# Gate and up products of a feed-forward block by Strassen's seven block products, in two groups of tokens

## The chip, the cores and the metric

The kernel runs on one core of a Trainium2 chip. The metric is the device time of one execution in microseconds (us). The core's engines are TensorE (PE, matrix products; PEld is its weight load), VectorE (DVE), ScalarE (ACT), GpSimd (POOL) and SyncE (SP, which here only issues DMA transfers). Each engine works its own instructions in order; semaphores tie the engines together. Matrix products accumulate in PSUM, all other tiles lie in SBUF.

## What is computed

One step of a streaming encoder layer for 1072 tokens (16 + 1024 + 32) of width 1024: two kinds of attention, an output projection, and a SwiGLU feed-forward part of hidden width 2816. Only the end of it is touched by the change:

```
def finish_layer(x, mixed, w_out, norm_ffn, w_gate, w_up, w_down):
    x = x + mixed @ w_out                     # second half of it in the stage looked at here
    h = rms_norm(x, norm_ffn)
    return x + (jax.nn.silu(h @ w_gate) * (h @ w_up)) @ w_down
y = rms_norm(finish_layer(...), final_norm)
```

Everything is in float32. A float32 factor is split into a high part and a low part of a shorter format (`split`, L65 to L67: ScalarE writes hi by a copy, VectorE writes lo as source minus hi), and one product is three matmuls: hi·hi, hi·lo, lo·hi (`mm3`, L117 to L121).

## The kernel before

Tokens lie along the columns. After attention, the stage `C` (from L770) holds the residual stream as `x2` and does, in this order: the second half of the output projection (L804 to L823, `psG<-A_hi,woh`), the operands of the feed-forward part (h without its per-token factor, as hi and lo in the four big tiles `A_hi`, `A_lo`, `B_hi`, `B_lo`, L829 and L830), the feed-forward part, and the last norm with the output.

The feed-forward part walks over 22 blocks f of 128 hidden units. Tokens stand in three chunks of 408, 408 and 256. For a block and a chunk `gate_up` issues 24 matmuls for the gate and 24 for the up product (eight slices of the 1024-wide contraction, three matmuls each), multiplies both by the token's norm factor `rb` (L849, L854), applies silu on ScalarE, multiplies (L855) and splits the result into `ah` and `al`. Then `down` works on the block before it: for each of eight output slices three matmuls into a PSUM tile `psD` (L861 to L863) and one VectorE addition of it to `x2` (L870). Gate, up and down share a ring of six PSUM tiles (`psG`, 2 KB per partition each). The weights of a block come by three transfers of 512 KB from SyncE's queue (L57), and are split in pieces of 1024 columns, one block ahead. GpSimd has no part in this until the last block, where it adds squares (L801) and scales outputs (L894).

What sets the order: engines run in program order, and a scheduler, which places the instructions of the loops above on each engine, has fixed it before the run. Tiles are taken from rings (`bufs`); an instruction that writes a tile waits for the last reader of the tile that stood there before.

## Time and profile before

| | |
|---|---|
| time, median of 3 runs | 1568.96 us (1565.36 to 1571.4) |
| the profiled execution | 1569.29 us |
| its span, first to last instruction | 1567.5 us |
| TensorE busy | 1494.9 us, 95% |
| VectorE busy | 978.5 us, 62% |
| ScalarE, GpSimd busy | 594.6 us, 215.8 us |
| TensorE's granted clock over the span | 0.99 of full speed |

The time of a run is 1.8 us longer than the span. Busy shares are averages over the attention part (up to about 716 us) and the stage `C` behind it; what holds in a stage is read from windows of that stage. A matmul's duration in the profile is longer than the distance to the next one, since matmuls overlap; the rate of TensorE is read from the distance between starts.

### The profile page before, as it was taken

What the parts mean: (1) busy time and instruction counts of PE and PEld (TensorE: products, weight loads), DVE (VectorE), ACT (ScalarE), POOL (GpSimd) and SP (SyncE); (2) the same over time, 40 slices, a digit from 0 to 9 for tenths busy, and PEclk for the clock granted to TensorE, in tenths of its full rate; (3) what the DMA queues carried; (4) which work ended last, traced back from release to release, by engine and by line L of the source; (5) the groups of instructions that cost most, each with busy time, mean ns of one, the idle gap of its engine ahead of it and who ended that gap; (6) DMA issues with size and microseconds to landing.
All of it is one profiled execution on the core that took longest, in us unless ns stands there. A gap on an engine that the chain in (4) does not pass through costs nothing.

```text
span 1567.5 us, 24204 instructions
## 1 busy us (share of the span) xinstructions
PE 1494.9 (95%) x9273; PEld 1432.9 (91%) x9273; DVE 978.5 (62%) x1843; ACT 594.6 (38%) x1204; POOL 215.8 (14%) x343
## 2 busy tenths in 40 slices
PE   7999998988898999998999999999999999999995
PEld 6999997777786988888999999999999999999995
DVE  8965535667767776775945556555655655655647
ACT  7444336666755665664612111111111111111124
POOL 1244141423232122110000000000000000000014
PEclk9999999999999999999999999999999999999998
DMA  6588666766867667625201111111111121111003
GB/s 192 172 279 277 198 205 203 249 200 176 237 205 205 176 162 189 165 84 187 62 28 41 46 63 55 41 41 41 41 41 41 41 64 54 45 41 41 27 1 113
DMA packets 88467, 185.27 MB, mean 118 GB/s; under 512 B 9818, under 2 KB 53786, under 8 KB 88260
## 3 DMA queue, kind: packets, MB, share of 16 engines
q1 hardware_dynamic: 71424, 129.44, 28.9%
q0 software_dynamic: 16928, 54.29, 9.9%
q8 instruction: 73, 1.20, 0.3%
q14 instruction: 42, 0.34, 0.1%
HBM read 125.02 MB, written 58.67 MB: 117 GB/s over the span
## 4 chain that ended last, share of the span: by engine, by line
PE 80%; DVE 6%; DMA 5%; ACT 4%; issue 3%; POOL 1%; DVEq 0%; SPq 0%; ACTq 0%; POOLq 0%
PE psG L120 11%; PE psG L119 11%; PE psG L121 11%; PE psD L862 5%; PE psD L863 5%; PE psD L861 5%; PE psS L568 4%; PE psT L630 3%; PE psA L121 3%; PE psA L119 3%; PE psA L120 3%; PE po L646 2%; PE po L647 1%; DMA sK<-es 1%; PE psG L816 1%
## 5 line engine op out<-in xcount | busy, mean ns | idle before, releaser
L870 DVE TENSOR_TENSOR x<-psD,x 128x408 f32<-128x408 f32 (+1 forms) x496 | 236.7, 524 | 5.7 <-PE psD L863 5.7
L119 PE MATMUL psG<-B_hi,gh 128*128 128x408 f32 (+1 forms) x528 | 172.8, 327 | 0.0
L119 PE MATMUL psG<-A_hi,gh 128*128 128x408 f32 (+1 forms) x528 | 172.6, 327 | 0.0
L120 PE MATMUL psG<-A_lo,gh 128*128 128x408 f32 (+1 forms) x528 | 172.6, 327 | 0.0
L120 PE MATMUL psG<-B_lo,gh 128*128 128x408 f32 (+1 forms) x528 | 172.5, 327 | 0.0
L863 PE MATMUL psD<-ah,dl 128*128 128x408 f32 (+1 forms) x528 | 172.1, 326 | 0.0
L121 PE MATMUL psG<-B_hi,gl 128*128 128x408 f32 (+1 forms) x528 | 171.8, 325 | 0.0
L121 PE MATMUL psG<-A_hi,gl 128*128 128x408 f32 (+1 forms) x528 | 171.8, 325 | 0.0
L862 PE MATMUL psD<-al,dh 128*128 128x408 f32 (+1 forms) x528 | 171.7, 325 | 0.0
L861 PE MATMUL psD<-ah,dh 128*128 128x408 f32 (+1 forms) x528 | 170.9, 325 | 0.1
L850 ACT ACTIVATE sl<-sl 128x408 f32<-128x408 f32 (+1 forms) x66 | 33.1, 503 | 354.6 <-DVE sl L849 354.6
L854 DVE TENSOR_TENSOR sq<-psG,rb 128x408 f32<-128x408 f32 (+1 forms) x66 | 35.0, 530 | 152.2 <-PE psG L121 152.1
L801 POOL TENSOR_TENSOR acc<-acc,sq 128x408 f32<-128x408 f32 x14 | 15.0, 1070 | 810.5 <-ACT sq L800 809.9
L571 DVE TENSOR_REDUCE nm<-psS 128x1 f32<-128x656 f32 (+2 forms) x144 | 104.2, 725 | 31.0 <-PE psS L568 29.8
L67 DVE TENSOR_TENSOR ptl<-psT,pth 128x512 fp32r<-128x512 f32 x192 | 104.2, 553 | 30.1 <-ACT pth L66 27.8
L66 ACT ACTIVATE pth<-psT 128x512 fp32r<-128x512 f32 (+4 forms) x208 | 98.5, 480 | 56.5 <-PE psT L630 49.4
L568 PE MATMUL psS<-b,a 128*128 128x328 f32 (+4 forms) x360 | 103.4, 338 | 9.1 <-ACT pb L576 5.5
L849 DVE TENSOR_TENSOR sl<-psG,rb 128x408 f32<-128x408 f32 (+1 forms) x66 | 35.0, 530 | 123.2 <-PE psG L121 123.2
L66 ACT ACTIVATE ah<-sl 128x408 fp32r<-128x408 f32 (+1 forms) x66 | 33.2, 503 | 188.5 <-DVE sl L855 121.4
L120 PEld LDWEIGHTS psG<-A_lo,gh 128*128 128x128 f32 x528 | 99.3, 188 | 0.5 <-issue 0.3
L861 PEld LDWEIGHTS psD<-ah,dh 128*128 128x128 f32 x528 | 99.2, 188 | 0.5 <-ACT ah L66 0.3
L119 PEld LDWEIGHTS psG<-A_hi,gh 128*128 128x128 f32 x528 | 99.2, 188 | 0.5 <-issue 0.2
(272 smaller groups left out, 3825.5 us busy)
## 6 DMA issues: line engine op xcount, KB each, us to landing
sg<-w_gu SPq DMA_DIRECT2D x44, 512.0 KB
a<-sQ SPq DMA_DIRECT2D x56, 268.0 KB
b<-sK SPq DMA_DIRECT2D x32, 396.0 KB
sg<-w_down SPq DMA_DIRECT2D x22, 512.0 KB
v<-sV SPq DMA_DIRECT2D x16, 512.0 KB
wst<-w_in SPq DMA_DIRECT2D x13, 512.0 KB
sV<-vt POOLq DMA_DIRECT2D x24, 256.0 KB, 3.9
sV<-A_hi POOLq DMA_DIRECT2D x24, 256.0 KB, 2.9
```

Of the source, the lines that this page charges most:

```text
L66: act.activation(hi, src, AF.Copy)
L67: eng.tensor_tensor(out=lo, in0=src, in1=f32(hi), op=ALU.subtract)
L119: pe.matmul(ps, whi(k), rhi(k), start=(k == 0), stop=False)
L120: pe.matmul(ps, whi(k), rlo(k), start=False, stop=False)
L121: pe.matmul(ps, wlo(k), rhi(k), start=False, stop=(k == K - 1))
L568: pe.matmul(out, qa[:K, t0:t0 + nq], kb[:K, k0 + c:k0 + c + w], start=(j == 0), stop=last)
L571: dve.tensor_reduce(out=nm[:nq, j:j + 1], in_=src, axis=AX.XY if len(src.shape) == 3 else AX.X, op=ALU.max, negate=True)
L630: pe.transpose(out=pt[:, 128 * g:128 * g + 128], in_=tiles[g][1][:, c:c + 128], identity=ident)
L861: pe.matmul(ps, dh[:, m], ah[:, cs], start=first and j == 0, stop=False)
L862: pe.matmul(ps, dh[:, m], al[:, cs], start=False, stop=False)
L863: pe.matmul(ps, dl[:, m], ah[:, cs], start=False, stop=last and j == len(parts) - 1)
L870: dve.tensor_tensor(out=x2[:, m, cs], in0=ps[:, :n], in1=x2[:, m, cs], op=ALU.add)
```

## The change

The matrix pair (gate, up) of a block is taken as a two-by-two block matrix: the contraction is halved (512 and 512), the outputs are gate and up, and the tokens are halved. Strassen's scheme (in Winograd's form) gives the four blocks of the result by seven block products in place of eight, with sums of blocks before and behind.

- Tokens are worked in two groups g of G = 536, each of two quarters of N = 268; a unit is a pair (g, f), so there are 44 units, and each block's weights are loaded twice.
- `w_sum` builds five of the seven weight operands of a unit by a GpSimd addition of two SBUF tiles (128x512, L811); two operands are the raw weights. `w_split` splits all seven, 512 columns each (hi in `gh` or `woh`, lo in `gl` or `wol`). The sums stand in the ring `wst` of two tiles. Both run about one unit ahead of the products (`ahead`).
- `h_make` writes the normalised h to SBUF and to DRAM; `h_first` and `h_last` build the seven token operands from it, the latter after the tiles `A_hi`, `A_lo` have been read for the last time as inputs of the output projection. For the second group this is done again at the end of the first one (`h_again`).
- `gate_up` issues seven products of 12 matmuls of 268 columns, in four PSUM tiles, and combines them (L981 to L1008); `ag` is the unit's result, and its split makes `ah` and `al`.
- `down` works on pairs of blocks, accumulated in PSUM: 48 matmuls, eight evictions (L1027) in a step, one step after each unit from f = 2 on. Its PSUM tiles `psD` are a ring of two of their own.
- The output projection goes by groups too; its eight weight tiles are loaded and split a second time. The end norms each quarter by itself (`final`).

```diff
@@ -508,9 +508,9 @@
     w_ring, w_next = [], [0]
 
     def out_weights(upto):
-        while w_next[0] < min(upto, 16):
+        while w_next[0] < min(upto, 24):
             stg, hi, lo = (wp.tile([128, 512], t, tag=g, name=g) for t, g in ((F32, "wst"), (FR, "woh"), (FR, "wol")))
-            load(stg.rearrange("p (k n) -> p k n", k=4), a["w_out"][w_next[0]])
+            load(stg.rearrange("p (k n) -> p k n", k=4), a["w_out"][w_next[0] if w_next[0] < 16 else w_next[0] - 8])
...
-        psN = C.enter_context(tc.tile_pool(name="psNF", bufs=2, space=PSUM))
+        psD = C.enter_context(tc.tile_pool(name="psD", bufs=2, space=PSUM))
+        N = T // 4
+        G = 2 * N
...
+        def w_sum(n):
+            if n >= 7 * len(units):
+                return
+            f, q = units[n // 7][1], n % 7
+            if q == 0:
+                up, gate = (wf.tile([128, 8, 128], F32, tag="sg", name="sg", bufs=3) for _ in range(2))
+                load(up, a["w_gu"][f, :, 1])
+                load(gate, a["w_gu"][f, :, 0])
+                raw[0] = (gate[:, 0:4], gate[:, 4:8], up[:, 0:4], up[:, 4:8])
+            a11, a12, a21, a22 = raw[0]
+            if q in (1, 2):
+                sums[n] = a11 if q == 1 else a22
+                return
+            x, y, op = {0: (a21, a22, ALU.add), 3: (a11, a12, ALU.add), 4: (a11, a22, ALU.add),
+                        5: (a21, a11, ALU.subtract), 6: (a12, a22, ALU.subtract)}[q]
+            s = wp.tile([128, 512], F32, tag="wst", name="wst").rearrange("p (k n) -> p k n", k=4)
+            pool.tensor_tensor(out=s, in0=x, in1=y, op=op)
+            sums[n] = s
+        def w_split(n):
+            if n >= 7 * len(units):
+                return
+            if n % 4 == 3:
+                hi, lo = (wp.tile([128, 512], FR, tag=t, name=t) for t in ("woh", "wol"))
+            else:
+                hi, lo = (wf.tile([128, 512], FR, tag=t, name=t, bufs=6) for t in ("gh", "gl"))
+            hi, lo = (t.rearrange("p (k n) -> p k n", k=4) for t in (hi, lo))
+            split(hi, lo, sums.pop(n))
+            quads[n] = (hi, lo)
...
+        def d_split(k):
+            if k >= len(steps):
+                return
+            _, p, h = steps[k]
+            sg = wf.tile([128, 2, 4, 128], F32, tag="dsg", name="dsg", bufs=1)
+            hi, lo = (wf.tile([128, 2, 4, 128], FR, tag=t, name=t) for t in ("dh", "dl"))
+            for j in range(2):
+                load(sg[:, j], a["w_down"][2 * p + j, :, 4 * h:4 * h + 4])
+            for j in range(2):
+                split(hi[:, j], lo[:, j], sg[:, j])
+            dws[k] = (hi, lo)
...
-                    for k in range(8):
-                        hi, lo = (t[:, k % 4, cs] for t in big[k // 4])
-                        act.activation(hi, x2[:, k, cs], AF.Copy, scale=g_ffn[:, k:k + 1])
-                        dve.scalar_tensor_tensor(lo, x2[:, k, cs], g_ffn[:, k:k + 1], f32(hi), ALU.mult, ALU.subtract)
-                    ps = psN.tile([128, 512], F32, tag="psn", name="psn")
-                    pe.matmul(ps[:, :n], ones, acc[:, cs], start=True, stop=True)
-                    rsqrt(rb[:, cs], ps, n, D, sqp)
...
+        def h_make(g, k):
+            h = ap_.tile([128, 2, G], F32, tag="hn", name="hn", bufs=2)
+            for j in range(2):
+                kk = k + 4 * j
+                dve.scalar_tensor_tensor(h[:, j], x2[g][:, kk], g_ffn[:, kk:kk + 1], accs[g], ALU.mult, ALU.mult)
+            put(sH[k, :, :, G * g:G * g + G], h)
+            return h
...
+        def h_first(h, k):
+            ct = ap_.tile([128, 3, N], F32, tag="ct", name="ct", bufs=1)
+            b = h.rearrange("p j (c n) -> p (j c) n", c=2)
+            dve.tensor_tensor(out=ct[:, 0], in0=b[:, 1], in1=b[:, 3], op=ALU.subtract)
+            dve.tensor_tensor(out=ct[:, 1], in0=b[:, 2], in1=b[:, 0], op=ALU.subtract)
+            yield
+            split(hB[0][:, 0:4:3, k], hB[1][:, 0:4:3, k], b[:, 0:4:3])
+            yield
+            split(hB[0][:, 1:3, k], hB[1][:, 1:3, k], ct[:, 0:2])
+            yield
+        def h_last(h, k):
+            ct = ap_.tile([128, 3, N], F32, tag="ct", name="ct", bufs=1)
+            b = h.rearrange("p j (c n) -> p (j c) n", c=2)
+            dve.tensor_tensor(out=ct[:, 0], in0=b[:, 0], in1=b[:, 3], op=ALU.add)
+            pool.tensor_tensor(out=ct[:, 1:3], in0=h[:, :, 0:N], in1=h[:, :, N:G], op=ALU.add)
+            yield
+            split(hA[0][:, 0:2, k], hA[1][:, 0:2, k], ct[:, 0:2])
+            yield
+            split(hA[0][:, 2, k], hA[1][:, 2, k], ct[:, 2])
+            yield
+        def h_again():
+            h = [h_load(1, 0)]
+            for k in range(4):
+                if k < 3:
+                    h.append(h_load(1, k + 1))
+                yield from h_first(h[k], k)
+                yield from h_last(h[k], k)
...
-            t1 = ap_.tile([128, 408], F32, tag="sl", name="sl")
-            t2 = sqp.tile([128, 408], F32, tag="sq", name="sq", bufs=2)
-            ps = product(0)
-            dve.tensor_tensor(out=t1[:, :n], in0=ps[:, :n], in1=rb[:, cs], op=ALU.mult)
-            silu[0] = act.activation(t1[:, :n], t1[:, :n], AF.Silu).ins
-            if between is not None:
-                between()
-            ps = product(1)
-            dve.tensor_tensor(out=t2[:, :n], in0=ps[:, :n], in1=rb[:, cs], op=ALU.mult)
-            dve.tensor_tensor(out=t1[:, :n], in0=t1[:, :n], in1=t2[:, :n], op=ALU.mult)
-            split(ah[:, cs], al[:, cs], t1[:, :n])
...
+        def gate_up(u):
+            g, f = units[u]
+            n0 = 7 * u
+            def product(ps, q, first):
+                hi, lo = quads.pop(n0 + q)
+                bh, bl = (t[:, q] for t in hB) if q < 4 else (t[:, q - 4] for t in hA)
+                for k in range(4):
+                    pe.matmul(ps[:, :N], hi[:, k], bh[:, k], start=first and k == 0, stop=False, skip_group_check=True)
+                    pe.matmul(ps[:, :N], hi[:, k], bl[:, k], start=False, stop=False, skip_group_check=True)
+                    pe.matmul(ps[:, :N], lo[:, k], bh[:, k], start=False, stop=(k == 3), skip_group_check=True)
+            def bank():
+                return psG.tile([128, 512], F32, tag="psG", name="psG")
+            def tmp(name):
+                return sqp.tile([128, N], F32, tag=name, name=name)
+            def ahead(q):
+                w_split(n0 + 7 + q)
+                w_sum(n0 + 8 + q)
+            pa, pb = bank(), bank()
+            product(pa, 0, True)
+            p0 = tmp("p0")
+            act.activation(p0, pa[:, :N], AF.Copy)
+            ahead(0)
+            product(pb, 1, True)
+            d = tmp("d")
+            dve.tensor_tensor(out=d, in0=pb[:, :N], in1=p0, op=ALU.subtract)
+            ahead(1)
+            product(pa, 2, False)
+            ahead(2)
+            product(pb, 3, False)
+            pc = bank()
+            product(pc, 4, True)
+            p4 = tmp("p4")
+            act.activation(p4, pc[:, :N], AF.Copy)
+            w = tmp("w")
+            dve.tensor_tensor(out=w, in0=pa[:, :N], in1=d, op=ALU.add)
+            dve.tensor_tensor(out=w, in0=w, in1=pb[:, :N], op=ALU.subtract)
+            g1 = tmp("g1")
+            silu[0] = act.activation(g1, pb[:, :N], AF.Silu).ins
+            ahead(3)
+            pd = bank()
+            product(pd, 5, True)
+            pool.tensor_tensor(out=d, in0=d, in1=p4, op=ALU.add)
+            ahead(4)
+            product(pc, 6, False)
+            ahead(5)
+            t = tmp("t")
+            dve.tensor_tensor(out=t, in0=pd[:, :N], in1=d, op=ALU.add)
+            dve.tensor_tensor(out=w, in0=pc[:, :N], in1=w, op=ALU.add)
+            act.activation(w, w, AF.Silu)
+            ag = sqp.tile([128, G], F32, tag="ag", name="ag")
+            dve.tensor_tensor(out=ag[:, N:G], in0=g1, in1=t, op=ALU.mult)
+            dve.tensor_tensor(out=ag[:, 0:N], in0=pa[:, :N], in1=w, op=ALU.mult)
+            ah, al = (t[:, f % 2] for t in (odd if f // 2 % 2 else spare))
+            split(ah, al, ag)
+            ahead(6)
+        def down(k, cs=(0, 1), norm=False, beside=iter(())):
+            g, p, h = steps[k]
+            dh, dl = dws[k]
+            ah, al = odd if p % 2 else spare
+            for c in cs:
+                for i in range(4):
+                    m = 4 * h + i
+                    ps = psD.tile([128, 512], F32, tag="psD", name="psD")
+                    for j in range(2):
+                        bh, bl = (t[:, j, N * c:N * c + N] for t in (ah, al))
+                        pe.matmul(ps[:, :N], dh[:, j, i], bh, start=(j == 0), stop=False)
+                        pe.matmul(ps[:, :N], dh[:, j, i], bl, start=False, stop=False)
+                        pe.matmul(ps[:, :N], dl[:, j, i], bh, start=False, stop=(j == 1))
+                    xs2 = x2[g][:, m, N * c:N * c + N]
+                    dve.tensor_tensor(out=xs2, in0=ps[:, :N], in1=xs2, op=ALU.add)
+                    if norm:
+                        square(g, m, c, pool if g == 0 else dve)
+                    next(beside, None)
...
+        for u, (g, f) in enumerate(units):
+            gate_up(u)
+            if g == 0 and f < 4:
+                h_make(1, f)
+            if f < 2 or f == 20:
+                continue
+            beside = iter(())
+            if f == 21 and g == 0:
+                beside = h_again()
+            for _ in range(1 if f < 20 else 2 if g == 1 else 4):
+                d_split(k + 1)
+                down(k, norm=f == 21 and steps[k][1] == NFF // 2 - 1, beside=beside)
+                k += 1
+            for _ in beside:
+                pass
+            if g == 1 and f in (2, 3):
+                final(0, f - 2)
+        d_split(k + 1)
+        for c in range(2):
+            down(k, (c,), norm=True)
+            down(k + 1, (c,), norm=True)
+            final(1, c)
```

TensorE around the seam between the products and the down step of a steady unit. Before, the down product of a chunk follows the last matmul of the up product; `DVE_49` and `Activation_49` are the semaphores of VectorE and ScalarE:

```order
L121 MATMUL psG<-B_hi,gl 128x408
L119 MATMUL psG<-B_hi,gh 128x408
L120 MATMUL psG<-B_lo,gh 128x408
L121 MATMUL psG<-B_hi,gl 128x408
L861 MATMUL psD<-ah,dh 128x408 [waits DVE_49,Activation_49]
L862 MATMUL psD<-al,dh 128x408
L863 MATMUL psD<-ah,dl 128x408
L861 MATMUL psD<-ah,dh 128x408 [waits DVE_49]
L862 MATMUL psD<-al,dh 128x408
```

Now, the piece from the end of the second `psD` tile of a step on, in the same view:

```order
L1025 MATMUL psD<-A_hi,dl 128x268
L960 MATMUL psG<-B_hi,woh 128x268
L961 MATMUL psG<-B_lo,woh 128x268
L962 MATMUL psG<-B_hi,wol 128x268
L960 MATMUL psG<-B_hi,woh 128x268
L961 MATMUL psG<-B_lo,woh 128x268
L1023 MATMUL psD<-A_hi,dh 128x268 [waits DVE_49]
L1024 MATMUL psD<-A_lo,dh 128x268
L1025 MATMUL psD<-A_hi,dl 128x268
L1023 MATMUL psD<-A_hi,dh 128x268
```

Two `psD` tiles are filled, five matmuls of the next unit's first product are drawn ahead, and the third `psD` tile waits for VectorE, which must have evicted the first.

VectorE in a stretch of the feed-forward part before, across the seam between two blocks (`x_8587` is the residual stream, `sg` a block's weights):

```order
L67 TENSOR_TENSOR dl<-sg,dh 128x1024
L870 TENSOR_TENSOR x_8587<-psD,x_8587 128x256
L67 TENSOR_TENSOR gl<-sg,gh 128x1024
L849 TENSOR_TENSOR sl<-psG,rb 128x408
L67 TENSOR_TENSOR gl<-sg,gh 128x1024
L854 TENSOR_TENSOR sq<-psG,rb 128x408
L870 TENSOR_TENSOR x_8587<-psD,x_8587 128x408
L855 TENSOR_TENSOR sl<-sl,sq 128x408
L870 TENSOR_TENSOR x_8587<-psD,x_8587 128x408 x2
L67 TENSOR_TENSOR al<-sl,ah 128x408
```

VectorE now, in one steady unit from the first combination behind product 2 on to the eviction of the first `psD` tile (`wst` are sums of weights from GpSimd, `psG` the products, `d` the tile to which GpSimd adds product 4):

```order
L991 TENSOR_TENSOR w_10937<-psG_10854,d_10886 128x268
L67 TENSOR_TENSOR wol_10943<-wst_10908,woh_10942 128x512
L992 TENSOR_TENSOR w_10937<-w_10937,psG_10855 128x268
L67 TENSOR_TENSOR gl_10963<-wst_10946,gh_10962 128x512
L67 TENSOR_TENSOR gl_10981<-wst_10966,gh_10980 128x512
L1003 TENSOR_TENSOR t_10986<-psG_10948,d_10886 128x268
L67 TENSOR_TENSOR gl_10996<-wst_10984,gh_10995 128x512
L1007 TENSOR_TENSOR ag_10990<-g1_10940,t_10986 128x268
L1004 TENSOR_TENSOR w_10937<-psG_10922,w_10937 128x268
L67 TENSOR_TENSOR wol_11095<-wst_11003,woh_11094 128x512
L1008 TENSOR_TENSOR ag_10990<-psG_10854,w_10937 128x268
L1027 TENSOR_TENSOR x20_8587<-psD_11014,x20_8587 128x268
```

Five low splits of weight sums stand between the combinations: four of the next unit, and one of the unit after it (`wol_11095`) just ahead of the last combination. The eviction of `psD` comes behind all of them.

GpSimd, which had nothing to do in the blocks before the last one, now works this sequence in the same unit, the last two rows being for the unit after the next:

```order
L811 TENSOR_TENSOR wst_10779<-sg_10775 128x512
L811 TENSOR_TENSOR wst_10908<-sg_10776 128x512
L811 TENSOR_TENSOR wst_10946<-sg_10776,sg_10775 128x512
L811 TENSOR_TENSOR wst_10966<-sg_10775,sg_10776 128x512
L811 TENSOR_TENSOR wst_10984<-sg_10776,sg_10775 128x512
L998 TENSOR_TENSOR d_10886<-d_10886,p4_10935 128x268
L811 TENSOR_TENSOR wst_11003<-sg_10999 128x512
L811 TENSOR_TENSOR wst_11132<-sg_11000 128x512
```

The unit's addition into `d` (L998) stands behind all five of a unit's weight sums, and the next sums follow it at once.

## Rows read from the trace of the kernel before

**Rows 1.** The page, part 1: busy time, share of the span and instructions of each engine

```profile
PE 1494.9 (95%) x9273; PEld 1432.9 (91%) x9273; DVE 978.5 (62%) x1843; ACT 594.6 (38%) x1204; POOL 215.8 (14%) x343
```

**Rows 2.** One stretch of the FFN by windows: busy us, instructions, clock, DMA share, GB/s

```profile
900.00:1000.00 100.00, 100.00 (x607) 99.81 (x606) 54.97 (x105) 16.05 (x24) 0.00 (x0) 1.00 0.15 48
```

**Rows 3.** SyncE's queue by time, 1005 to 1045 us: start us, us, engine, transfer

```profile
1007.10 0.33 SPq L57 DMA_DIRECT2D sg<-w_down  x1
1012.16 29.15 SPq L57 DMA_DIRECT2D sg<-w_gu  x2
1042.45 0.33 SPq L57 DMA_DIRECT2D sg<-w_down  x1
```

**Rows 4.** TensorE by time: the first matmul of the stage

```profile
716.73 0.42 PE L816 MATMUL psG<-A_hi,woh 128*128 128x408 f32 x1 [1.36 <-DVE raw L691]
```

**Rows 5.** TensorE by time: the last matmul of the last down product

```profile
1548.17 0.28 PE L863 MATMUL psD<-ah,dl 128*128 128x256 f32 x1
```

**Rows 6.** TensorE by time, matmuls of 256 and of 408 columns: start us, us, name

```profile
1000.38 0.28 PE L861 MATMUL psD<-ah,dh 128*128 128x256 f32 x1
...
1003.09 0.28 PE L863 MATMUL psD<-ah,dl 128*128 128x256 f32 x1
1003.21 0.35 PE L119 MATMUL psG<-A_hi,gh 128*128 128x408 f32 x1
...
1012.15 0.35 PE L861 MATMUL psD<-ah,dh 128*128 128x408 f32 x1
```

**Rows 7.** A window of 1 us behind the load issued at 1012.16 (columns as in rows 2)

```profile
1015.00:1016.00 1.00, 1.00 (x7) 1.00 (x6) 1.00 (x3) 0.00 (x0) 0.00 (x0) 1.00 0.11 45
```

**Rows 8.** All engines by time, 468.4 to 471 us: GpSimd and VectorE side by side

```profile
468.86 1.27 POOL L67 TENSOR_TENSOR wol<-wst,woh 128x512 fp32r<-128x512 f32 x1 [2.48 <-ACT woh L66]
469.14 1.38 DVE L504 TENSOR_TENSOR et<-et,et 128x358 f32<-128x358 f32 x1
```

**Rows 9.** VectorE groups by shape, 690 to 1568 us: count, busy us, mean ns, idle before

```profile
L870 DVE TENSOR_TENSOR x<-psD,x 128x408 f32<-128x408 f32 x336 | 176.6, 575 | 5.7 <-PE psD L863 5.7
L870 DVE TENSOR_TENSOR x<-psD,x 128x256 f32<-128x256 f32 x160 | 60.1, 418 | 0.0
L67 DVE TENSOR_TENSOR wol<-wst,woh 128x512 fp32r<-128x512 f32 x6 | 4.1, 686 | 0.1
```

**Rows 10.** VectorE and GpSimd by time, 1549 to 1554.5 us

```profile
1549.78 0.98 DVE L914 TENSOR_TENSOR acc<-acc,sq 128x512 f32<-128x512 f32 x1
1552.03 1.53 DVE L914 TENSOR_TENSOR acc<-acc,sq 128x512 f32<-128x512 f32 x1
...
1548.14 7.66 POOL L894 TENSOR_TENSOR x<-x,acc 128x408 f32<-128x408 f32 x6 [9.56 <-DVE acc L115]
```

**Rows 11.** GpSimd groups by shape, the whole span

```profile
L801 POOL TENSOR_TENSOR acc<-acc,sq 128x408 f32<-128x408 f32 x14 | 15.0, 1070 | 810.5 <-ACT sq L800 809.9
L67 POOL TENSOR_TENSOR wol<-wst,woh 128x512 fp32r<-128x512 f32 x10 | 13.0, 1302 | 28.0 <-ACT woh L66 27.9
```

**Rows 12.** VectorE and GpSimd by time, 1523 to 1526 us

```profile
1523.21 0.58 DVE L870 TENSOR_TENSOR x<-psD,x 128x408 f32<-128x408 f32 x1 [0.52 <-PE psD L863]
...
1522.47 4.52 POOL L801 TENSOR_TENSOR acc<-acc,sq 128x408 f32<-128x408 f32 x4
```

**Rows 13.** ScalarE groups by shape, 690 to 1568 us (columns as in rows 9)

```profile
L66 ACT ACTIVATE woh<-wst 128x512 fp32r<-128x512 f32 x6 | 3.8, 625 | 9.3 <-PE psG L817 9.3
```

**Rows 14.** TensorE by time: matmuls behind two idle stretches of the attention part

```profile
335.13 0.58 PE L474 MATMUL psF<-woh,A_hi 128*128 128x256 f32 x1 [2.10 <-DVE A_hi L67]
...
482.62 0.55 PE L630 MATMUL psT<-ident,pa 128*128 128x128 f32 x3 [2.00 <-DVE ptm L635]
```

**Rows 15.** Windows of 3 us behind these two

```profile
335.00:338.00 3.00, 2.87 (x12) 2.87 (x13) 2.48 (x5) 1.86 (x6) 0.54 (x1) 0.50 0.35 129
483.00:486.00 3.00, 2.72 (x17) 2.34 (x16) 2.94 (x8) 2.08 (x4) 0.69 (x1) 1.00 0.82 273
```

More of the change, by code (lines that the diff above doesn't have):

```diff
@@ new lines, in trunk @@
+        for g in range(2):
+            for m in range(8):
+                load(x2[g][:, m], sX2[128 * m:128 * m + 128, G * g:G * g + G])
+        raw, sums, quads = [None], {}, {}
+        units = [(g, f) for g in range(2) for f in range(NFF)]
+        def w_sum(n):
[16 more added lines that the diff above has]
+            sums[n] = s
@@ new lines, in w_split @@
+        def w_split(n):
[8 more added lines that the diff above has]
+            quads[n] = (hi, lo)
+        steps = [(g, p, h) for g in range(2) for p in range(NFF // 2) for h in range(2)]
@@ L947, in _fm @@
+        d_split(k + 1)
+        for c in range(2):
+            down(k, (c,), norm=True)
+            down(k + 1, (c,), norm=True)
+            final(1, c)
 def _fm(w, k):
```

198 lines of the change are left out of this document (70 added, 128 removed).

## The prediction

> **What bounds the kernel now.** I read the page first: TensorE is busy 95% of the span, VectorE 62%, GpSimd 14% [rows 1]. A mean says little, so the second view is a stretch of the feed-forward part by windows: TensorE 100 of 100 us at full granted clock, VectorE 55, ScalarE 16, GpSimd nothing, DMA 15% [rows 2]. The reader is to see that nothing but TensorE's rate bounds this stage, that VectorE has 45% to spare, and that GpSimd has never been asked to work beside it here. A block lasts 35.35 us, from one load of `w_down` to the next [rows 3]. The stage runs from 716.7 us [rows 4] to the last down matmul at 1548.3 [rows 5]; the 19.2 us behind it are the last norm and the output.
>
> **The products.** From start to start a matmul of 256 columns takes (1003.09 - 1000.38)/23 = 0.1178 us and one of 408 (1012.15 - 1003.21)/48 = 0.1863 [rows 6]. The line between them gives 0.1232 us for 268 columns (an estimate; 0.121 to 0.126). The stage after has 44 x 84 = 3696 matmuls of products, 2112 of down and 384 of the output projection: 6192 x 0.1232 = 763 us. Before, 22 x 35.35 = 778 us went to the feed-forward part alone; its 5808 matmuls are now 716. So the change offers some 60 us, and everything else below is what it pays.
>
> The Trainium skill, TensorE: Matmul & The Clock Gate, section "Wait — 56ns, not 53.3ns?", gives the columns over 2.4 GHz plus 2.5 ns as the distance of warm matmuls, thus 114 ns for 268 columns and a sum 56 us lower than mine. The trace has 117.8 ns where that gives 109 for 256 columns, so I keep the rows.
>
> **The loads** double for `w_gu` and `w_down`; a 512 KB load issued at 1012.16 [rows 3] has ended its traffic early in the microsecond after 1015 [rows 7], so 3.1 us, and at 15% DMA share [rows 2] twice as many are hidden, but for one in the seam below.
>
> **What two engines do to each other.** This is the cost that the added GpSimd sums bring, and the trace shows it. A GpSimd addition ran from 468.86 to 470.13; a VectorE operation with both inputs in SBUF that started at 469.14 took 1.38 us [rows 8], where 0.52 is what its 358 columns cost by the line between 0.418 and 0.575 [rows 9]. It ended 0.39 us after GpSimd did: it stood still until then. In the tail such a pair alternates: `acc<-acc,sq` of 512 columns takes 0.98 and 1.53 us where an undisturbed one of that width takes 0.69 [rows 9, 10], and the six GpSimd operations beside it 7.66/6 = 1.28 [rows 10] against 1.07 for the same shape [rows 11]. Operations that read PSUM and SBUF are free of it: the `x` eviction takes 0.58 amid four GpSimd additions that run through [rows 12].
>
> The Trainium skill, SBUF — State Buffer, section "Who interferes with whom", states this as an exclusive lock: VectorE with two SBUF inputs and GpSimd reading SBUF share a port, and the second to issue waits for the whole of the first. The trace agrees: 0.39 us left after release in place of 0.52.
>
> So a 512-wide low split (0.69 undisturbed) takes until GpSimd's end plus 0.55 (0.39 x 512/358), and a GpSimd sum lasts 1.30 [rows 11], or some 1.15 counted from VectorE's end.
>
> **A steady unit.** TensorE: 132 x 0.1232 = 16.26 us. VectorE: nine low splits at 0.61 from start to start (0.69 less 0.08 of overlap), one of 536 columns at 0.63, 15 operations of 268 at 0.35: 11.3 us. GpSimd: five sums of 1.30 and one addition of 0.70 (1.07 x 268/408): 7.2. Added up as if one always excluded the other, VectorE needs 18.5 us, over TensorE's 16.26. What decides is where they meet, and that is the seam in the order: `psD` has two tiles, so TensorE, 17 matmuls (2.1 us) after product 6, waits for the first eviction, which VectorE does last, behind the combinations. I walk it in us from the end of product 3, with 0.2 from a product's end to its reader's start, 0.06 for a semaphore, and 0.6 for a ScalarE high split [rows 13]. A split of a next unit's operand reuses the tiles of eight operands earlier, so operand q waits for product q - 1 of this unit.
>
> - Sum 5 follows low split 3 and runs 0.13 to 1.41. Low split 4 (high part done 0.8) waits for it: 1.41 to 1.96.
> - Sum 6 runs 2.02 to 3.30; low split 5 (high part 2.3) waits: to 3.85. Then GpSimd's addition into `d`: to 4.45. `t` needs it: 4.5 to 4.85 (its product was done at 3.0).
> - Sum 0 of the unit after the next follows at once: 4.45 to 5.70. Low split 6 waits: to 6.25. The first half of `ag`: to 6.55; `w` with product 6: to 6.9.
> - Sum 3 of that unit, released by low split 6, gets the port at 6.55: to 7.70. Low split 0 waits: to 8.25. Second half of `ag`: 8.55. First eviction: 8.9.
> - TensorE wanted it at 4.44 (end of product 6) + 2.1 = 6.54. It idles 2.4 us.
>
> Without any lock the same walk has `t` at 3.95, low split 6 at 4.6, sum 0 at 4.85, its high part 5.5, low split 0 at 6.15, eviction 6.9: 0.4 us. If sum 3 comes after low split 0, it is 1.7. Which of these comes first hangs on the gate's load, issued when sum 6 is done (3.35) and landed 3.1 later, at 6.45: most often just in time for 6.55. I take 2.2 and keep 0.4 and 3.0 as ends. 36 units with a down step and the two at the groups' ends: 38 x 2.2 = 84 us (15 to 114).
>
> **TensorE's clock.** A 2.10 us wait at 333 us was followed by 3 us at a granted clock of 0.50 (1.2 GHz); a 2.00 us wait at 480 us by 1.00 (2.4 GHz) [rows 14, 15]. My 2.2 us stand at that edge. Three microseconds at half rate lose 1.5. I take it for one unit in five: 12 us (0 to 57).
>
> **The rest of the stage.** Start: h can be made only when the norm of group 0 is there, about 31 us in (24 of products, eviction, norm chain), and from there to the end of unit 0's `ag` VectorE has 84 instructions, 39 us by the same distances, so 70 at the earliest, while TensorE's 468 matmuls take 58; with some GpSimd collisions I take 22 us (12 to 35). The second group's operands beside the last down steps of the first: VectorE 31 us against 34, now with GpSimd's squares and sums: 10 (3 to 22). Norms of group 0 within group 1: 4 (0 to 8). The first matmuls after 716.7 at the lower clock: 2. Tail: 21 for 19.2, eight scalings on VectorE alone (17 to 25).
>
> Sum: 716.7 + 763 + 22 + 84 + 12 + 10 + 4 + 2 + 21 = 1634.7, with 1.8 outside the span 1636.5. The profiled run, 1569.3, lies 0.3 over the median, so 1636.
>
> **The rivals.**
>
> The engines miss each other: stalls at 0.4, start 18, seam of the groups 5, no fall of the clock: 716.7 + 763 + 18 + 15 + 5 + 4 + 2 + 21 + 1.8 = 1547, faster. For it: 45% of VectorE's time is idle, and its PSUM operations do not collide. Against it: in the order, each sum is released by a low split, just ahead of another one. It decides at a stall of 1.0 us a unit: below, the kernel is not slower. Chance 0.13 for faster, 0.09 for a stall about there (1561 to 1577).
>
> The gate's load comes late, so low split 0 goes ahead of sum 3: stall 1.7, no fall of the clock, 1636 - 19 - 12 = 1605. For it: the 0.1 us between the two. Chance 0.20.
>
> The clock falls behind every stall: 57 in place of 12, 1681. For it: the 2.10 us row; against: TensorE is dense for 16 us between these waits, and was not there. Chance 0.15.
>
> My forecast has the remaining 0.43.
>
> **The numbers.** About 0.5% (8 us) is what a measurement of this kernel can tell from no change: faster is below 1561, slower above 1577. Slower 0.43 + 0.20 + 0.15 = 0.78, same 0.09, faster 0.13. The range leaves out the faster case and the far end of the clock's: 1560 to 1695.
>
> **What would show it.** Matmuls of products start 0.123 us apart. `L67` low splits with a `wst` input have a mean well over 0.69, about 1.2 us, while `L1027` evictions keep 0.43; `L811` means 1.3 to 1.5. TensorE's idle time before `L1023` is put down to VectorE's eviction, some 2 us once in a unit, units are 18 to 19 us apart, and windows show VectorE busy about 80%. It is wrong if `L67` stays at 0.69, if units come in 16.3 to 17 us, or if the waits stand in front of other matmuls, such as product 3 or 4.

## The result and the profile after

The kernel with Strassen's products takes 1686.97 us (median of four runs, 1686.13 to 1688.74), the kernel before 1569.43 in the same session: a ratio of 1.0754, interval 1.0731 to 1.0777. It is 117.5 us slower, 51 more than the forecast of 1636 and within its range. The profiled run is 1686.86 us with a span of 1685.1.

Page, part 1 (columns as in [rows 1]):

```profile
PE 1482.7 (88%) x10423; PEld 1398.4 (83%) x10423; DVE 1267.1 (75%) x2224; ACT 808.4 (48%) x1659; POOL 573.9 (34%) x616
```

A stretch of the steady units by windows (columns as in [rows 2]):

```profile
900.00:1100.00 200.00, 180.27 (x1418) 176.91 (x1417) 161.07 (x268) 79.77 (x149) 87.60 (x66) 1.00 0.25 87
```

TensorE, which was busy 100 of 100 us [rows 2], is busy 180 of 200; VectorE has gone from 55% to 81% and GpSimd from nothing to 44%. The clock is full: the loss is waiting. What TensorE waited for there:

```profile
PE psD L1023 <- DVE x L1027: 19.7, 13, 1.7
```

All 19.7 us are waits of a down product for the eviction of a `psD` tile, none for another cause. The groups of the stage (group | busy, mean ns | idle before) say why VectorE is late; the first two and the fourth answer to [rows 9, 11], the third is the eviction:

```profile
L67 DVE TENSOR_TENSOR gl<-wst,gh 128x512 fp32r<-128x512 f32 x165 | 176.3, 1070 | 20.9 <-ACT gh L66 20.9
L67 DVE TENSOR_TENSOR dl<-dsg,dh 128x512 fp32r<-128x512 f32 x88 | 61.4, 734 | 5.3 <-ACT dh L66 1.6
L1027 DVE TENSOR_TENSOR x<-psD,x 128x268 f32<-128x268 f32 x352 | 147.7, 432 | 68.1 <-PE psD L1025 67.0
L811 POOL TENSOR_TENSOR wst<-sg 128x512 f32<-128x512 f32 x220 | 303.8, 1389 | 460.5 <-DVE gl L67 260.3 <-DVE wol L67 98.1 <-DMA sg<-w_gu 45.1
```

The low splits of weight sums (the VectorE half of a split, L67) take 1070 ns in the mean; those of `w_down`, the same shape and mostly apart from GpSimd's sums, 734; the eviction, which reads PSUM, kept its 432. One steady unit in order of time, VectorE (start us, us, line, [idle before it]):

```profile
1050.90 0.43 DVE L992 TENSOR_TENSOR w<-w,psG 128x268 f32<-128x268 f32 x1 [0.18 <-PE psG L962]
1051.50 1.14 DVE L67 TENSOR_TENSOR gl<-wst,gh 128x512 fp32r<-128x512 f32 x1 [0.17 <-ACT gh L66]
1052.98 1.58 DVE L67 TENSOR_TENSOR wol<-wst,woh 128x512 fp32r<-128x512 f32 x1 [0.34 <-ACT woh L66]
1055.22 0.44 DVE L1003 TENSOR_TENSOR t<-psG,d 128x268 f32<-128x268 f32 x1 [0.66 <-PE psG L961]
1055.58 1.41 DVE L67 TENSOR_TENSOR gl<-wst,gh 128x512 fp32r<-128x512 f32 x1
1056.91 0.42 DVE L1007 TENSOR_TENSOR ag<-g,t 128x268 f32<-128x268 f32 x1
1057.26 0.42 DVE L1004 TENSOR_TENSOR w<-psG,w 128x268 f32<-128x268 f32 x1
1057.60 0.68 DVE L67 TENSOR_TENSOR gl<-wst,gh 128x512 fp32r<-128x512 f32 x1
1058.23 0.44 DVE L1008 TENSOR_TENSOR ag<-psG,w 128x268 f32<-128x268 f32 x1
1058.59 0.77 DVE L1027 TENSOR_TENSOR x<-psD,x 128x268 f32<-128x268 f32 x2
```

GpSimd and TensorE beside it:

```profile
1050.80 1.30 POOL L811 TENSOR_TENSOR wst<-sg 128x512 f32<-128x512 f32 x1 [9.49 <-DVE gl L67]
1052.72 1.30 POOL L811 TENSOR_TENSOR wst<-sg 128x512 f32<-128x512 f32 x1 [0.63 <-DVE gl L67]
1053.97 1.22 POOL L998 TENSOR_TENSOR d<-d,p 128x268 f32<-128x268 f32 x1
1055.15 1.28 POOL L811 TENSOR_TENSOR wst<-sg 128x512 f32<-128x512 f32 x1
1058.53 3.00 POOL L811 TENSOR_TENSOR wst<-sg 128x512 f32<-128x512 f32 x2 [2.10 <-DMA sg<-w_gu]
```

```profile
1057.15 0.28 PE L961 MATMUL psG<-B_lo,gh 128*128 128x268 f32 x1
1059.07 0.40 PE L1023 MATMUL psD<-ah,dh 128*128 128x268 f32 x1 [1.63 <-DVE x L1027]
```

The reader is to see the pairs. The sum of 1050.80 ends at 1052.10 and the low split that started at 1051.50 at 1052.64; the sum of 1052.72 ends at 1054.02 and the split of 1052.98 at 1054.56; 1056.43 and 1056.99. Each split ends 0.54 to 0.56 us after its sum. One split runs alone, at 1057.60, and takes 0.68: the sum that should have stood beside it waited 2.10 us for the gate's load. So the eviction comes at 1058.59 and TensorE idles 1.63 us. The clock around that wait (columns as in [rows 2]):

```profile
1057.00:1060.00 3.00, 1.37 (x11) 1.16 (x10) 2.97 (x7) 1.18 (x3) 1.47 (x2) 1.00 0.50 194
1059.00:1062.00 3.00, 2.93 (x21) 2.76 (x22) 2.30 (x6) 0.36 (x1) 2.54 (x2) 1.00 0.01 3
```

It stayed at 1.00, 2.4 GHz. Counted from one last `ag` (L1008) to the next, units are mostly 18.4 us apart and sometimes 19.4; the mean of 17 between 849.85 and 1170.58 us is 18.87. In the units of 19.4 a second wait of 0.8 us follows. It has the same cause: the low split of `ag` reads two SBUF tiles as well, meets the two sums that the gate's load had held back, and takes 1.86 us, so the evictions behind it are late too:

```profile
1038.78 2.52 POOL L811 TENSOR_TENSOR wst<-sg 128x512 f32<-128x512 f32 x2 [1.72 <-DMA sg<-w_gu]
1040.01 1.86 DVE L67 TENSOR_TENSOR A_lo<-ag,A_hi 128x536 fp32r<-128x536 f32 x1
1042.28 0.39 PE L1023 MATMUL psD<-ah,dh 128*128 128x268 f32 x1 [0.83 <-DVE x L1027]
```

The stage's pieces that are no steady unit: start to the first `hn`, on to the end of unit 0, the groups' boundary, the last down products:

```profile
718.00:768.60 50.60, 44.53 (x306) 41.70 (x307) 32.35 (x71) 20.14 (x46) 2.94 (x2) 0.93 0.58 197
768.60:820.30 51.70, 34.49 (x213) 31.61 (x212) 48.88 (x85) 25.14 (x50) 22.52 (x18) 0.83 0.37 122
...
1189.40:1252.60 63.20, 49.06 (x366) 46.09 (x366) 57.82 (x96) 31.44 (x65) 34.73 (x30) 1.00 0.20 66
1637.70:1670.30 32.60, 24.83 (x174) 23.29 (x172) 24.25 (x59) 12.36 (x24) 0.00 (x0) 0.91 0.15 51
```

Unit 0 ends 101 us behind the stage's first matmul (718.81), where the 468 matmuls of the projection and of unit 0 need 57.7: VectorE is busy 49 of the second 51.7 us, TensorE stands idle for 23 in both, and the clock was granted at 0.93 and 0.83.

### The profile page after: what moved, and what is told of

Same layout as the page of the kernel before. It is cut to its first block, busy times and chain, and to the rows that moved or that the text cites. A ratio compares the mean times of both kernels' runs of the same rounds, so it can differ in the third digit from the quotient of the medians.

```text
span 1685.1 us, 28432 instructions
## 1 busy us (share of the span) xinstructions
PE 1482.7 (88%) x10423; PEld 1398.4 (83%) x10423; DVE 1267.1 (75%) x2224; ACT 808.4 (48%) x1659; POOL 573.9 (34%) x616
## 4 chain that ended last, share of the span: by engine, by line
PE 57%; DVE 23%; DMA 6%; ACT 5%; issue 5%; POOL 3%; SPq 0%; ACTq 0%; DVEq 0%; POOLq 0%
PE psG L960 6%; PE psG L961 6%; PE psG L962 6%; DVE gl L67 5%; PE psD L1023 4%; PE psS L568 3%; PE psD L1024 3%; PE psD L1025 3%; PE psT L630 3%; PE psA L119 2%; PE psA L121 2%; PE psA L120 2%; DVE wol L67 2%; PE po L646 2%; DVE A_lo L67 1%
## 5 line engine op out<-in xcount | busy, mean ns | idle before, releaser
L811 POOL TENSOR_TENSOR wst<-sg 128x512 f32<-128x512 f32 x220 | 303.8, 1389 | 460.5 <-DVE gl L67 260.3
L1027 DVE TENSOR_TENSOR x<-psD,x 128x268 f32<-128x268 f32 x352 | 147.7, 432 | 68.1 <-PE psD L1025 67.0
L67 DVE TENSOR_TENSOR gl<-wst,gh 128x512 fp32r<-128x512 f32 x165 | 176.3, 1070 | 20.9 <-ACT gh L66 20.9
L1023 PE MATMUL psD<-A_hi,dh 128*128 128x268 f32 x384 | 118.7, 309 | 50.7 <-DVE x L1027 50.4
L960 PE MATMUL psG<-B_hi,gh 128*128 128x268 f32 x528 | 152.7, 289 | 11.9 <-ACT p L977 8.0
L962 PE MATMUL psG<-B_hi,gl 128*128 128x268 f32 x528 | 152.8, 289 | 0.0
L961 PE MATMUL psG<-B_lo,gh 128*128 128x268 f32 x528 | 151.7, 287 | 0.0
L1023 PE MATMUL psD<-ah,dh 128*128 128x268 f32 x320 | 97.1, 303 | 38.3 <-DVE x L1027 38.3
L67 DVE TENSOR_TENSOR ptl<-psT,pth 128x512 fp32r<-128x512 f32 x192 | 104.2, 553 | 30.8 <-ACT pth L66 28.4
L1023 PEld LDWEIGHTS psD<-A_hi,dh 128*128 128x128 f32 x384 | 73.8, 192 | 60.3 <-DVE x L1027 59.6
L960 PE MATMUL psG<-A_hi,gh 128*128 128x268 f32 x396 | 114.2, 289 | 5.6 <-ACT p L989 4.1
L961 PE MATMUL psG<-A_lo,gh 128*128 128x268 f32 x396 | 113.8, 287 | 0.2 <-DVE A_lo L67 0.2
L962 PE MATMUL psG<-A_hi,gl 128*128 128x268 f32 x396 | 113.8, 288 | 0.0
```

Of the source, the lines that this page charges most:

```text
L67: eng.tensor_tensor(out=lo, in0=src, in1=f32(hi), op=ALU.subtract)
L811: pool.tensor_tensor(out=s, in0=x, in1=y, op=op)
L960: pe.matmul(ps[:, :N], hi[:, k], bh[:, k], start=first and k == 0, stop=False, skip_group_check=True)
L961: pe.matmul(ps[:, :N], hi[:, k], bl[:, k], start=False, stop=False, skip_group_check=True)
L962: pe.matmul(ps[:, :N], lo[:, k], bh[:, k], start=False, stop=(k == 3), skip_group_check=True)
L1023: pe.matmul(ps[:, :N], dh[:, j, i], bh, start=(j == 0), stop=False)
```

## The experiments

Two theories stand at first. **Lock**: GpSimd's sums and VectorE's low splits hold each other up, and that makes the eviction late. **Buffer**: VectorE is late in any case and two `psD` tiles are too few to cover it. Each run's ratio is to the kernel before, run beside it.

**The sums write but don't read.** This kernel leaves out the five weight sums: two fills of a constant (526 ns each) stand in their place. Unlike the sums, the fills don't wait for the loads of weights either.

```diff
-            pool.tensor_tensor(out=s, in0=x, in1=y, op=op)
+            for _ in range(2):
+                pool.memset(s, 0.001)
```

> The five GpSimd additions of weights in a unit become two fills of the same tile each: GpSimd writes it and reads nothing from SBUF; who waits for whom stays. The weights' sums are left out of the computation. Theory (VectorE and GpSimd exclude each other where both read SBUF): the low splits fall back from 1.07 to 0.69 us, the stall in front of the third psD tile from 1.8 to 0.1 to 0.5 us, a unit from 18.4 to 18.9 to 16.5 to 16.9, and the whole by 70 to 100 us, to 1590 to 1615. Rival (the chain through GpSimd and the ring of two sums is too long, whatever it reads): units stay at 18 us or more and the time over 1665.

Measured: 1573.16 us, ratio 1.0025 (1.0013 to 1.0038); units 16.77 apart. VectorE's low split from 900 to 1100 us, GpSimd's fill from 900 to 1170, and the window that answers to the one above:

```profile
L67 DVE TENSOR_TENSOR gl<-wst,gh 128x512 fp32r<-128x512 f32 x45 | 31.1, 691 | 10.3 <-ACT gh L66 10.3
```

```profile
L812 POOL MEMSET wst<- 128x512 f32 x150 | 79.0, 526 | 151.6 <-DVE gl L67 104.6 <-DVE wol L67 41.5
```

```profile
900.00:1100.00 200.00, 199.16 (x1575) 196.51 (x1574) 152.13 (x298) 89.50 (x168) 73.52 (x132) 1.00 0.30 96
```

GpSimd is busy 37% of that stretch and still the split takes 691 ns in place of 1070, and TensorE doesn't wait once for `psD`. So it is what GpSimd reads, not that it works, that holds VectorE up. That the fills are shorter and wait for no load can have helped the whole, but not the length of a single split. The whole came out below the expected range, since start and boundary gained as well.

**The sums on VectorE.** The same work, all of it on one engine:

```diff
-            pool.tensor_tensor(out=s, in0=x, in1=y, op=op)
+            dve.tensor_tensor(out=s, in0=x, in1=y, op=op)
...
-            pool.tensor_tensor(out=d, in0=d, in1=p4, op=ALU.add)
+            dve.tensor_tensor(out=d, in0=d, in1=p4, op=ALU.add)
```

> All five weight sums and the addition into d go from GpSimd to VectorE; everything is computed. VectorE's own work in a unit grows from 11.3 to 14.7 us (5 x 0.61 + 0.35). Theory (exclusion): low splits at 0.69 us, units at 16.3 to 17.2, the whole 1590 to 1630. Rival (VectorE's load is what binds, and more of it makes it worse): units at 18.4 or more, 1690 or more.

Measured: 1567.78 us, 0.9991 (0.9981 to 1.0002); units mostly 16.5 apart. The low split and the window from 900 to 1100 us:

```profile
L67 DVE TENSOR_TENSOR gl<-wst,gh 128x512 fp32r<-128x512 f32 x46 | 31.4, 683 | 0.8 <-ACT gh L66 0.5
```

```profile
900.00:1100.00 200.00, 200.00 (x1603) 198.83 (x1602) 188.86 (x388) 90.26 (x169) 0.00 (x0) 1.00 0.31 103
```

VectorE is busy 94% and TensorE 100%: giving VectorE more work, five sums and an addition a unit, took 119 us off the kernel after (1686.97 - 1567.78, each beside the same kernel before). That is the second support for the lock, with the computation whole. The units came as expected; the whole is below the expected 1590 to 1630, since the start and the units on either side of the groups' boundary gained here too. An engine at 94% kept up.

**A third `psD` tile**, taken from `psG`:

```diff
-        psG = C.enter_context(tc.tile_pool(name="psG", bufs=6, space=PSUM))
-        psD = C.enter_context(tc.tile_pool(name="psD", bufs=2, space=PSUM))
+        psG = C.enter_context(tc.tile_pool(name="psG", bufs=5, space=PSUM))
+        psD = C.enter_context(tc.tile_pool(name="psD", bufs=3, space=PSUM))
```

> Three psD tiles in place of two, five psG in place of six. In the order TensorE then does three psD tiles and no matmuls of the next product ahead of its wait, 18 matmuls in place of 17. Theory (the first eviction is late, behind VectorE's chain): the wait shrinks by 0.1 us a unit only, the whole stays within 10 us of 1687. Rival (the ring of two tiles is the limit): 0.74 us less a unit, 1650 to 1662.

Measured: 1674.8 us, 1.0672 (1.0649 to 1.0694), units mostly 18.2 to 19.2 apart, the low split still at 1093 ns, and TensorE's busy time as in the kernel after:

```profile
900.00:1100.00 200.00, 179.69 (x1402) 175.76 (x1401) 161.20 (x268) 80.63 (x149) 86.28 (x66) 0.99 0.26 86
```

The buffer theory falls: 12 of 118 us, somewhat more than the 10 allowed for. TensorE's wait in a unit is mostly 1.52 us in place of 1.64, the 0.1 that the lock's walk gives. The mean of units between 850 and 1171 us stays (18.90; 18.87 in the kernel after). The gain lies in group 1's units (18.5 in place of 19.1) and in the last down products (28.9 us in place of 32.5).

**The gate's load earlier.** The wait of 2.10 us for it could be the cause of the late eviction, or what kept one more collision away. The block's weights come in quarter tiles, six in the ring in place of three halves, so that a quarter is loaded as soon as one is free:

```diff
-                up, gate = (wf.tile([128, 8, 128], F32, tag="sg", name="sg", bufs=3) for _ in range(2))
...
+                for j, h in ((1, 0), (0, 0), (1, 4), (0, 4)):
+                    part.append(wf.tile([128, 4, 128], F32, tag="sg", name="sg", bufs=6))
+                    load(part[-1], a["w_gu"][f, :, j, h:h + 4])
```

> The weights of gate and up come as four quarter tiles of 256 KB in a ring of six, ordered so that the gate's halves take tiles that are free two microseconds earlier. Sum 3 of the unit after the next, now held back by its transfer until after low split 0, then starts ahead of it. Theory (exclusion): low split 0 waits for that sum, the first eviction comes 0.7 to 0.9 us later, units at 19.1 to 19.6, the whole 1705 to 1725: earlier weights, slower kernel. Rival (late transfers are part of the loss): units shorter than 18.4, under 1680.

Measured: 1752.94 us, 1.1179 (1.1142 to 1.1216): 66 slower than the kernel after, units 20.7 apart, the low split at 1267 ns. The end of a unit, GpSimd, VectorE and TensorE:

```profile
1014.88 2.85 POOL L812 TENSOR_TENSOR wst<-sg 128x512 f32<-128x512 f32 x2 [0.79 <-DVE t L1004]
1015.07 1.53 DVE L1008 TENSOR_TENSOR ag<-g,t 128x268 f32<-128x268 f32 x1
1017.00 1.28 DVE L67 TENSOR_TENSOR gl<-wst,gh 128x512 fp32r<-128x512 f32 x1
1019.02 0.59 PE L1024 MATMUL psD<-A_hi,dh 128*128 128x268 f32 x1 [2.70 <-DVE x L1028]
```

```profile
1019.00:1022.00 3.00, 2.98 (x13) 2.98 (x14) 1.62 (x3) 0.31 (x1) 0.63 (x1) 0.50 0.00 0
```

With its data there the sum runs, and now `ag` takes 1.53 us and the split 1.28. TensorE waits 2.70 us, and behind that the clock is granted at 0.50, 1.2 GHz. The expectation, 1705 to 1725, had left this fall out of its sum: the mean clock from 900 to 1100 us was 0.91, which is 1.9 us of each unit. The wait itself grew by 1.0 us, where 0.7 to 0.9 had been expected.

**The unit's last split issued later**, so that a combination goes ahead of it:

```diff
+            seen = dve.tensor_tensor(out=w, in0=pc[:, :N], in1=w, op=ALU.add).ins
...
-            ahead(6)
+            with tc.issue_after(seen):
+                ahead(6)
```

> The changed kernel with one edge of order: a unit's low split 6 (and its high one) is issued behind the VectorE addition of product 6 into w (L1004). The sums stay on GpSimd. Theory (exclusion in the seam): w and its silu no longer wait behind low split 6, which stands still until GpSimd's sum 0 is done; by the walk the first eviction ends 0.5 to 0.6 us earlier, units fall from 18.4 to 17.8 to 18.0 us, the whole to 1660 to 1672. Rival (what counts is VectorE's work and GpSimd's added up, wherever they meet): units and time as in the changed kernel, 1680 to 1692.

Measured: 1670.68 us, 1.0637 (1.0616 to 1.0659), units 18.5 in the mean. What TensorE waited for between 900 and 1100 us:

```profile
PE psD L1024 <- DVE x L1028: 16.6, 22, 1.1
```

The waits are shorter and more: 16.6 us in place of 19.7. The whole came within the theory's 1660 to 1672, the units did not come down to its 17.8 to 18.0. Another order, like another tile, moves the wait and keeps most of it.

**The weight sums on VectorE, the addition into `d` left on GpSimd** (the first of the two edits of the run with all sums on VectorE):

> As e2, but the addition of product 4 into d stays on GpSimd: one GpSimd operation in a unit that reads SBUF in place of none (e2) or six (the changed kernel). Theory (exclusion, where they meet counts): it meets a low split or a sum of weights and costs at most one wait of 0.5 to 0.7 us in front of the first eviction; units 16.5 to 17.0, the whole 1566 to 1590. Rival (any GpSimd addition in the seam brings the whole stall): units of 17.8 or more, over 1620.

Measured: 1586.23 us, 1.0102 (1.0084 to 1.0119), units 17.0. VectorE and GpSimd where they meet, and TensorE's waits from 900 to 1100 us:

```profile
1051.83 1.20 POOL L998 TENSOR_TENSOR d<-d,p 128x268 f32<-128x268 f32 x1 [16.04 <-DVE wst L811]
1052.43 1.15 DVE L811 TENSOR_TENSOR wst<-sg 128x512 f32<-128x512 f32 x1
```

```profile
PE psD L1023 <- DVE x L1027: 3.6, 10, 0.5
```

One GpSimd addition a unit costs 18 us of the kernel (1586.23 - 1567.78, two sessions), as the lock has it: VectorE's sum ends 0.55 us after GpSimd's addition.

**The start.** With all sums on VectorE the steady part is free of waits, and yet the kernel is only level with before. There unit 0 ends 97 us behind the stage's first matmul, the boundary takes 46, the end 33. Three runs on top of it look for the start's limit. First, `w_out` weights on a larger ring, asked for two steps earlier:

```diff
+                hi, lo = (late[0].tile([128, 512], FR, tag=g, name=g, bufs=6) for g in ("gh", "gl"))
...
-                    out_weights(8 + 8 * g + m + 2)
+                    out_weights(8 + 8 * g + m + 4)
```

> With all sums on VectorE (e2), the split weights of the output projection's second half take the ring of six tiles of the products (gh, gl) in place of a ring of two, and are asked for two tiles earlier. In e2 TensorE waited 15 us for such weights before the first unit was done. Theory R (that ring costs the start its time): the end of unit 0 comes 10 to 15 us earlier, the whole 1552 to 1560. Theory S (VectorE's own work sets the start): under 4 us, 1563 to 1569.

Measured: 1569.21 us, 0.9992 (0.998 to 1.0005), unit 0 after 98.0 us. No effect on the time: between 714 and 820 us TensorE's waits for these weights fell from 15.3 us to 4.5, and others came in their place.

Second, the squares of the first norm summed by TensorE (matmuls with a matrix of ones for each row tile) in place of VectorE, and the norm of group 0 issued ahead of the other group's projection:

```diff
-                    square(g, m, c, dve)
+                    square_pe(g, m, c)
+                if g == 0 and u0 == 6:
+                    for c in range(2):
+                        rstd(0, c)
```

> With all sums on VectorE (e2), the squares for the norm in front of the feed-forward part are added up by TensorE (matmuls with ones, in float32) in place of 28 VectorE additions (9.8 us). Theory S (VectorE's own work sets the start, TensorE idles there): the end of unit 0 comes 5 to 10 us earlier, the whole 1557 to 1563. Theory R (the weights' ring sets it): under 3 us, or slower by the 14 us that TensorE gets added.

Measured: 1566.38 us, 0.9975 (0.9959 to 0.9991), unit 0 after 94.7 us: 2.4 less, where 5 to 10 were expected. The way from the stage's first matmul to the end of unit 0, with the sums on VectorE and then here, and the added matmuls:

```profile
715.70:812.80 97.10, 78.60 (x529) 74.52 (x530) 78.23 (x163) 45.12 (x96) 9.03 (x8) 0.88 0.49 167
722.50:817.20 94.70, 87.94 (x585) 81.15 (x585) 67.74 (x135) 45.35 (x96) 10.58 (x8) 0.95 0.51 171
L857 PE MATMUL psn<-sq,ones 128*128 128x268 f32 x64 | 18.9, 407 | 1.0 <-ACT sq L856 0.7
```

TensorE's idle time there fell from 18.5 us to 6.8. So most of what TensorE waited for is gone, and most of the gain was spent on the added matmuls, 18.9 us of TensorE's busy time.

Third, both of these and the squares of the last norm on TensorE too:

> e6 and e7 together, and the sums of squares of the last norm also by TensorE, which takes 14 GpSimd additions (0.89 us each) out of the seam between the groups and 14 VectorE additions out of the end. If each of these is what holds its place: start 10 to 20 us, seam 3 to 6, end 4 to 8 less than e2, the whole 1538 to 1552, which would beat both kernels. If TensorE's added matmuls (64 of 0.45 us, 29 us) lie on the path: 1565 or more.

Measured: 1573.08 us, 1.0014 (1.0 to 1.0028): not the hoped-for case but the other one, 1565 or more. The boundary took 52.7 us (46.0 with the sums on VectorE), the end 34.7 (32.6). Both grew although VectorE had less to do. The windows of the boundary, first with the sums on VectorE, then in this run, and the norm's matmuls in the latter:

```profile
1139.00:1185.00 46.00, 40.88 (x304) 37.98 (x303) 45.74 (x84) 23.34 (x49) 18.89 (x18) 1.00 0.24 77
```

```profile
1139.00:1185.00 46.00, 40.60 (x267) 36.31 (x267) 39.43 (x79) 24.62 (x49) 5.34 (x4) 1.00 0.26 83
L862 PE MATMUL psn<-sq,ones 128*128 128x268 f32 x32 | 10.2, 406 | 0.1
```

GpSimd's 18.89 us fall to 5.34 and VectorE's 45.74 to 39.43. TensorE is as busy as there (40.60 and 40.88 us) but gets through 267 matmuls in place of 304, and 32 of these are the added ones, 10.2 us of its busy time. So it doesn't wait more; it pays for the sums of squares itself, as the second case of the expectation has it. What else holds the boundary was not separated.

**The end.** On top of the run with the first norm's squares on TensorE, the last down products take their PSUM from the ring of six, and the first half's scalings go behind the second half's evictions:

```diff
-                    ps = psD.tile([128, 512], F32, tag="psD", name="psD")
+                    ps = bank("psD") if last else psD.tile([128, 512], F32, tag="psD", name="psD")
...
+            down(k, (c,), norm=True, last=True)
+            down(k + 1, (c,), norm=True, last=True)
+            if c == 1:
+                scale(1, 0)
+            final(1, c, c == 0)
```

> e7 (all sums on VectorE, first norm's squares added by TensorE) with two edits at the end: the last down products take their PSUM tiles from the ring of six, and the eight scalings of the third quarter are issued behind the evictions of the fourth. In e2 TensorE waited 6.2 us there for evictions. If that wait and the scalings hold the end: 3 to 6 us less than e7, 1560 to 1564, faster than both kernels. If VectorE's work sets the end, which it still has to do: within 1 us of e7.

Measured: 1560.93 us, 0.9939 (0.9922 to 0.9956): below both kernels. TensorE's waits in the last down products, with the sums on VectorE and then here:

```profile
PE psD L1023 <- DVE x L1027: 6.2, 4, 2.9
```

```profile
PE psn L865 <- DVE acc L848: 4.4, 1, 4.4
```

The four waits for `psD` are gone (the one that is left belongs to the last norm), and the way from the last unit to the last down matmul is 21.9 us in place of 32.6; behind that matmul the tail takes 18.5 us in place of 14.8. So more PSUM tiles, or the later scalings, did help here; the two edits were made together and their shares are not shown.

## Why the prediction was right, and where its sizes were off

- **Direction and cause were right.** The lock between GpSimd's sums and VectorE's low splits makes the change a loss; two runs that take the reading off GpSimd bring it to 1573 and 1568. The signs came as named: low splits of 1070 ns, evictions of 432, sums of 1389, the waits before L1023, units of 18.87 us and VectorE at 81%. A blocked split ended 0.54 to 0.56 us after GpSimd's sum, predicted as 0.55 from the 0.39 of 358 columns [rows 8]. The Trainium skill, SBUF — State Buffer, section "Who interferes with whom", states that a VectorE instruction with two SBUF inputs contends with a GpSimd instruction that reads SBUF, and that the lock is exclusive. The trace agrees, with these 0.54 to 0.56 us.
- **The steady unit.** With the end of product 3 at 1050.70 (0.2 ahead of its reader, as in the walk), the ten steps from sum 5 to `w` came within about 0.1 us: low split 4 done at 1.94 us (1.96 predicted), low split 5 at 3.86 (3.85), the addition into `d` at 4.49 (4.45), low split 6 at 6.29 (6.25), `w` at 6.98 (6.9). The one open place, whether the gate's load is in time for the sum of the next unit, fell to the rival: it was late, low split 0 ran alone and the stall was 1.8 (1059.07, where the last matmul's start and one distance give 1057.27) where I took 2.2. In the sum it came out even: the units are 18.87 - 16.26 = 2.6 us over the products, in which the matmul's distance of 0.1241 us in place of 0.1232 is 0.1. All steady units of both groups, group 0's norms among them, lie some 99 us over their products; 84 + 12 + 4 = 100 had been set aside. This evenness is luck in part: the first wait was smaller than taken, the clock fell in three of these units only, and the second wait, behind the split of `ag`, where the walk had already ended, made up for it.
- **What the walk did not see.** It ends at the first eviction, and so has no second wait. Otherwise the two runs that move the wait bear it out: it gave 0.1 us a unit for a third tile, and the wait fell from 1.64 to 1.52; it gave 0.5 to 0.6 for the other order, and the units fell by 0.4. Beside the walk stood a sum, 11.3 us of VectorE and 7.2 of GpSimd when one always excludes the other, 18.5 us, and the units of both runs are near it. But the two engines' common time is not what bounds the unit: laid over each other in the trace, their instructions cover 178 of the 200 us from 900 to 1100, so for a tenth of the time neither works. And with the same work the wait grew from 1.6 to 2.6 us where the loads came earlier. What counts is which operations meet in front of the evictions.
- **The clock.** 12 us were set aside; behind waits of 1.6 us it did not fall. The prediction read an edge between waits of 2.00 and 2.10 us from [rows 14, 15]. The kernel after shows that the length of a wait alone doesn't decide: it stayed at 1.00 behind waits of 2.62 us (871.08) and 3.06 us (1205.63), and fell behind one of 1.90 (1459.18):

```profile
1205.70:1208.70 3.00, 3.00 (x24) 3.00 (x25) 2.93 (x9) 0.71 (x2) 1.38 (x1) 1.00 0.04 16
1459.20:1462.20 3.00, 2.98 (x14) 2.67 (x15) 2.88 (x4) 0.27 (x1) 1.56 (x2) 0.61 0.02 8
```

Where every wait was made longer, with the gate's load earlier, the clock fell in every unit between 870 and 1210 us.

- **The failed terms are the edges.** Start: 22 predicted and 2 for the lower clock, 53 found (44 to the end of unit 0, 9 in the two units behind). From the windows above: 519 matmuls at 0.1241 are 64.4 us, busy were 79.0; by the granted clock up to 12 us of the 102 were lost to the lower level (0.07 of 50.6 and 0.17 of 51.7), where 2 had been set aside; TensorE was idle for 23.3; the 51 matmuls that are not unit 0's or the projection's are 6.3. I had counted VectorE's work from the norm on, but the first `hn` came 50 us into the stage, not 31. The last eviction of group 0's projection ends 32.5 us in (751.31), and behind it VectorE has splits for the first units and evictions of the other group between the norm's steps, up to 768.6. From there to the end of unit 0 it took 52 us where 39 had been counted. The boundary: 10 predicted, 27 found (46.4 us where 34 had been, and 6 and 8 on either side). With the sums on VectorE the 46.4 are still 46.0, so the weight sums are not what holds it; what does stays open. The last down products: nothing predicted, 9 found, for four evictions that came late. The tail was shorter: 14.8 behind the last down matmul where 21 was taken. These are +29, +17, +9 and -6: 49 of the 51 us. The stage's first matmul came 2 us later.
- **The rivals, and luck.** The late load (1605) is what the steady unit did, a stall of 1.8 us where that rival has 1.7, but its whole is 82 us short, for the edges. The clock behind every stall (1681) is nearest in number, and its cause did not happen. That 1687 lies inside the range at all is luck: the top of the range had been left open for the clock, and the edges used that room. "The engines miss each other" (1547) did not happen, but is what the sums on VectorE give: units of 16.5 us, and even there the edges eat nearly all of the 60 us that the products offer: 97 - 58 at the start, 46 - 34 at the boundary, 33 - 24 at the end.

## What to carry to other kernels

Before work is given to an idle GpSimd, ask which of the VectorE operations that it will stand beside read two SBUF tiles while it reads SBUF too: here the sums on the idle engine cost 119 us more than on VectorE, which ran at 94% with them. A wait that ends at an eviction need not be a lack of tiles; see first what stands ahead of the eviction on its engine and why that is late. Here it was blocked splits, and another tile or order only moved the wait. And work out the edges of a stage (start, seam of groups, end) with the same care as its steady unit: here they were 49 of the error's 51 us.
